# Moving the up phase's stores from SyncE's queue to the queues of GpSimd and ScalarE in a one-core decoder trunk

## The chip, the cores and the metric

The kernel runs on one core of a Trainium2 chip. A core has a matrix engine (TensorE, PE in the profile, with PEld for its weight loads), VectorE (DVE), ScalarE (ACT), GpSimd (POOL) and SyncE (SP), each working through its own list of instructions in order. Transfers between the chip's memory (HBM) and the on-chip buffer are DMAs. An engine issues one with an instruction in its own list, and the core's 16 DMA engines move the bytes. Engines wait for each other, and for DMAs, by semaphores: a waiting instruction holds all that stands behind it in its engine's list.

The metric is the device time of one execution in microseconds; smaller is better.

## The reference

One layer of a decoder trunk over 1024 positions of 1024 channels, in float32:

```python
h = layer_norm(x, ln_in_g, ln_in_b)
u = h @ w_in                       # conformer GLU | ssm z | ssm x,B,C | dt | gate_a | gate_b
y_a = conformer_branch(...)        # depthwise convolution of 31 taps
y_b = ssd_branch(...)              # Mamba-2, chunks of 128 positions
mix = (sigmoid(gate_a) * y_a + sigmoid(gate_b) * y_b) @ w_o
h = layer_norm(DN_ALPHA * h + mix, ln1_g, ln1_b)
# ConvFFN: the part that the change touches, and what follows it
u = causal_dwconv(h @ w_up, dw_w, dw_b)      # w_up (1024, 5632), 3 taps
gate, val = split(u, 2)
ffn = (silu(gate) * val) @ w_down            # w_down (2816, 1024)
h = layer_norm(DN_ALPHA * h + ffn, ln2_g, ln2_b)
```

## The kernel before

Each product runs as three float32r matmuls (`mm3`, lines 163 to 168), on a high part and a low part of each operand. So every weight tile that is loaded from HBM is first cast by ScalarE (the high part), then VectorE subtracts to give the low part, and only then can TensorE use it.

The kernel works in stages: the mixers and the combination for each half of the positions, the output projection, then the feed-forward network, in an up phase and a down phase.

*The up phase* (lines 1094 to 1107) makes 22 pairs of a gate and a value column block, numbered j. It saves multiplications: the positions and the channels are split in two, and each block product of 2 x 2 is made from seven smaller products. Two of the seven need only the first half of the positions and go ahead: `up_first(j)` (lines 806 to 814) multiplies with `b11` and then adds `b21` on top in the same accumulator. After each of the two, ScalarE copies the accumulator to a tile `first` (line 813; four such tiles) and line 814 stores it to HBM (`first_scr`). Eight such products run ahead (`LEAD`, line 1100); the other fourteen are strewn between the later ones. `up_rest(j)` (lines 839 to 907) makes the other five products:

- `up_weights` loads two raw weight tiles, `ra` and `rb` (lines 826 and 827), and VectorE makes sums of them.
- Lines 848 and 849 load the two stored products of `up_first(j)` again.
- ScalarE and VectorE bring together the partial results in `ug` and `uv` (lines 856 to 868), GpSimd clears their two leading columns (850 and 851), then the convolution of three taps and the gate follow in tiles of the tag `fo` (lines 870 to 896; three tiles).
- The result goes to HBM: for the lower eleven blocks the first half (line 899, 256 KB), for the upper eleven the whole tile (line 901, 512 KB) and two combinations of it with the lower block (lines 906 and 907, 512 and 256 KB).

*The down phase* (`down`, lines 909 to 1065) loads these tiles and the down weights again in steps (`load`): `dr` (lines 958 to 966) holds one step's operands, `c` (line 998) weights that are kept for later steps. The two rows of the last norm are loaded by line 203.

All DMAs, loads and stores alike, are issued by SyncE (`SY`).

*What sets the order.* The kernel is written in program order, but the list of each engine is laid out at build time by a planner (`schedule_with_timeline_sim`, line 1203). It goes forward in a modelled time with its own costs for every instruction, and gives an engine that is free the ready instruction of the highest priority. Priority is program order, with blocks moved ahead by `tc.high_priority(offset=...)`: weight loads and casts by 4000 or 2000 instructions (lines 150, 819, 955). Stores have no such offset. A tile's memory is given out again when its last reader is through, a store included. On the chip each list then runs in the planned order, whatever the real durations.

Of the kernel before, what the change touches and what calls it, by code (L numbers as in the profile page):

```python
# [55 lines left out]
def kernel(  # L56
# [15 lines left out]
    V, A, G, TE, SY = nc.vector, nc.scalar, nc.gpsimd, nc.tensor, nc.sync  # L72
# [14 lines left out]
    def bank(which):  # L87
        n_ps[0] += 1
        pl, tag = (pacc, "acc") if which else (psm, "sm")
        return pl.tile([P, 512], F32, tag=tag, name=f"{tag}{n_ps[0]}")  # L90
# [47 lines left out]
    first_scr = [dram.tile([2, P, HALF], F32, name=f"first_scr{j}") for j in range(NF)]  # L138
    NK = NF // 2
    b11_scr = [dram.tile([P, HALF], F32, name=f"b11_scr{k}") for k in range(NK)]  # L140
    t1_scr = [dram.tile([P, HALF], F32, name=f"t1_scr{k}") for k in range(NK)]
    b2_scr, t32_scr = (
        [dram.tile([P, T], F32, name=f"{n}_scr{k}") for k in range(NK)] for n in ("b2", "t32")
    )
# [4 lines left out]
    def weights(src, name, pl=None, eng=None, bufs=None):  # L149
        with tc.high_priority(offset=4000):  # L150
            st = wst.tile([P, D], F32, tag="st", name=f"st_{name}")
            SY.dma_start(st, src)
            w = (pl or wsp).tile([P, 2, D], F32R, tag="w", bufs=bufs, name=f"w_{name}")
            A.copy(w[:, 0, :], st)  # L154
            (eng or V).tensor_tensor(  # L155
                out=w[:, 1, :], in0=st, in1=w[:, 0, :].bitcast(F32), op=ALU.subtract
            )
        return w
# [557 lines left out]
    def product(ps, w, xs, first):  # L716

        for k in range(4):
            mm3(
                ps,  # L720
                lambda i: w(i)[:, k * P : (k + 1) * P],
                lambda i: xs(i)[:, k, :],
                first and k == 0,
                k == 3,
                not first,
            )
# [79 lines left out]
    def up_first(qp, bl, j):  # L806

        w = weights(wup[2 * j], f"ue{j}")
        ps = bank(1)
        for q, block in enumerate(("b11", "b21")):  # L810
            product(ps, lambda i: w[:, i, q * HALF : (q + 1) * HALF], bl[block], q == 0)
            f = qp.tile([P, HALF], F32, tag="first", bufs=4, name=f"first{q}_{j}")
            A.copy(f, ps)  # L813
            SY.dma_start(first_scr[j][q], f)

    def up_weights(upp, j):


        with tc.high_priority(offset=2000):
            r1, r2 = (  # L820
                wst.tile([P, D], F32, tag="st", name=f"r{n}{j}")
                if j % 2
                else upp.tile([P, D], F32, tag="raw", bufs=2, name=f"r{n}{j}")
                for n in "ab"
            )
            SY.dma_start(r1, wup[2 * j])
            SY.dma_start(r2, wup[2 * j + 1])
            a11, a12, a21, a22 = r1[:, :HALF], r1[:, HALF:], r2[:, :HALF], r2[:, HALF:]
            s3 = upp.tile([P, HALF], F32, tag="s3", name=f"s3_{j}")
            V.tensor_tensor(out=s3, in0=a11, in1=a21, op=ALU.add)  # L830
            V.tensor_tensor(out=a21, in0=a21, in1=a22, op=ALU.add)
            V.tensor_tensor(out=a11, in0=a21, in1=a11, op=ALU.add)
            V.tensor_tensor(out=a12, in0=a12, in1=a11, op=ALU.add)
            w24 = split_pair(wsp, r1, f"s24_{j}")
            w10 = split_pair(wsp, r2, f"s10_{j}")
            w3 = split_pair(upp, s3, f"s3_{j}", HALF, 2)
        return w24, w10, w3

    def up_rest(upp, bl, j, before):

        w24, w10, w3 = up_weights(upp, j)
        ug, uv = (
            upp.tile([P, T + 32], F32, tag="u", bufs=3, name=f"f{n}{j}") for n in ("ug", "uv")
        )
        s = upp.tile([P, HALF], F32, tag="s", bufs=2, name=f"s{j}")
        SY.dma_start(s, first_scr[j][0])
        SY.dma_start(ug[:, 2 : 2 + HALF], first_scr[j][1])
        G.memset(ug[:, :2], 0.0)  # L850
        G.memset(uv[:, :2], 0.0)
        ps, pz = bank(0), bank(0)
        early, late = slice(2, 2 + HALF), slice(2 + HALF, 2 + T)
        seeded = j > 1
        if seeded:
            A.copy(ps, s)
        product(ps, lambda i: w24[:, i, :HALF], bl["t2"], not seeded)
        if not seeded:
            V.tensor_tensor(out=ps, in0=s, in1=ps, op=ALU.add)
        A.copy(s, ps)  # L860
        product(pz, lambda i: w3[:, i], bl["t3"], True)
        product(ps, lambda i: w10[:, i, :HALF], bl["t1"], False)
        A.copy(uv[:, late], ps)  # L863
        V.tensor_tensor(out=uv[:, late], in0=pz, in1=uv[:, late], op=ALU.subtract)
        product(pz, lambda i: w10[:, i, HALF:], bl["t4"], False)
        V.tensor_tensor(out=uv[:, early], in0=pz, in1=s, op=ALU.subtract)
        product(ps, lambda i: w24[:, i, HALF:], bl["b22"], False)
        A.copy(ug[:, late], ps)
        os = []
        j = j // 2 + j % 2 * NK  # L870
        for jj, u in ((j, ug), (NF + j, uv)):
            o = upp.tile([P, T], F32, tag="o", bufs=3, name=f"fo{jj}")
            wc = PC_FW + 3 * jj
            A.activation(
                out=o, in_=u[:, 2 : 2 + T], func=AF.Identity, scale=pc[:, wc + 2 : wc + 3]
            )
            for k in range(2):
                V.scalar_tensor_tensor(
                    out=o,
                    in0=u[:, k : k + T],  # L880
                    scalar=pc[:, wc + k : wc + k + 1],
                    in1=o,
                    op0=ALU.mult,
                    op1=ALU.add,
                )
            os.append(o)
        og, ov = os
        A.activation(out=og, in_=og, func=AF.Silu, bias=pc[:, PC_FB + j : PC_FB + j + 1])
        V.scalar_tensor_tensor(
            out=ov,  # L890
            in0=ov,
            scalar=pc[:, PC_FB + NF + j : PC_FB + NF + j + 1],
            in1=og,
            op0=ALU.add,
            op1=ALU.mult,
        )
        early, late = slice(0, HALF), slice(HALF, T)
        if j < NK:
            SY.dma_start(b11_scr[j], ov[:, early])
            return ov  # L900
        SY.dma_start(b2_scr[j - NK], ov)
        a, b, t = before, ov, og
        V.tensor_tensor(out=t[:, early], in0=a[:, late], in1=b[:, late], op=ALU.subtract)
        V.tensor_tensor(out=a[:, late], in0=a[:, early], in1=a[:, late], op=ALU.subtract)
        V.tensor_tensor(out=t[:, late], in0=t[:, early], in1=a[:, early], op=ALU.subtract)
        SY.dma_start(t32_scr[j - NK], t)
        SY.dma_start(t1_scr[j - NK], a[:, late])

    def down(upp, dp, g, b):

# [183 lines left out]
    def firsts_to(n):  # L1094
        nonlocal n_first
        while n_first < min(n, NF):
            up_first(qp, bl, n_first)
            n_first += 1
# [5 lines left out]
    for j in range(NF):  # L1104
        firsts_to(LEAD + (j + 1) * (NF - LEAD) // (NF - 1))
        before = up_rest(upp, bl, j, before)
# [103 lines left out]
```

## Time and profile before

| | us |
|---|---|
| median of three runs (2031.75 to 2035.14) | 2033.81 |
| the profiled execution | 2034.61 |
| its span, first to last instruction | 2032.8 |
| TensorE busy | 1974.6 (97%) |
| VectorE busy | 1696.9 (83%) |
| ScalarE busy | 1031.2 (51%) |
| GpSimd busy | 147.3 (7%) |

The granted clock of TensorE is 0.991 of full speed on average. All DMAs together move 297.14 MB.

In the rows of the profile, `L814` is line 814 of the kernel; `SPq` is SyncE's queue, whose instructions issue DMAs and are not counted as busy. `first_scr<-first` names what is written and what is read. A row of a timeline gives the start (us from the span's start), the duration in us, the engine, the line, the operation, and how many were merged (x2); brackets hold the engine's idle time just before, and who ended it. A row of waits gives who waited for whom, the total in us, how many times, and the longest. The tiles `fo` are those of lines 872 to 896, `w_s` the cast weights of `up_weights`, `w_ue` those of `up_first`, `w_dn` those of the down phase. `b_scr` stands for `b11_scr` and `b2_scr`, `t_scr` for `t1_scr` and `t32_scr`.

### The profile page before, as it was taken

The numbers are of one execution on the slowest core, as the hardware profiler recorded it, in microseconds if no ns is written. First come the engines' busy times: TensorE is split into PE (matmuls) and PEld (weight loads), VectorE is DVE, ScalarE is ACT, GpSimd is POOL, SyncE is SP. The second block draws the span as 40 slices with busy tenths as digits, with TensorE's granted clock in tenths as the row PEclk, the third lists the DMA queues.
The fourth block names the chain that finished last, engine by engine and source line by source line (L and its number), as shares of the span: only waits on it lengthen the run. The fifth ranks groups of instructions, "written<-read, shape, count | busy, mean of one in ns | idle before, by whom it ended". The sixth has DMA issues, their size and how long they took to land.

```text
span 2032.8 us, 24888 instructions
## 1 busy us (share of the span) xinstructions
PE 1974.6 (97%) x9164; PEld 1624.8 (80%) x9164; DVE 1696.9 (83%) x2243; ACT 1031.2 (51%) x1489; POOL 147.3 (7%) x125
## 2 busy tenths in 40 slices
PE   6999999999999999999999999999999999979997
PEld 6888887888788888888888888887888888768865
DVE  7599999989766868999998976596788888879669
ACT  4465654556453265665454635264555555544323
POOL 2010101001400000100000131010000000000000
PEclk9999999999999999999999999999999999989999
DMA  6212233232545532222323253575455454775564
GB/s 219 93 63 94 78 102 106 99 104 100 165 129 197 203 106 75 88 84 84 122 86 114 98 170 126 182 247 208 158 169 191 163 190 166 277 289 184 161 210 147
DMA packets 110858, 297.14 MB, mean 146 GB/s; under 512 B 12560, under 2 KB 12560, under 8 KB 110736
## 3 DMA queue, kind: packets, MB, share of 16 engines
q1 hardware_dynamic: 110736, 295.55, 43.4%
q8 instruction: 72, 1.18, 0.3%
q14 instruction: 50, 0.41, 0.1%
HBM read 241.50 MB, written 54.00 MB: 145 GB/s over the span
## 4 chain that ended last, share of the span: by engine, by line
PE 72%; DVE 19%; DMA 5%; issue 3%; ACT 1%; SPq 0%; DVEq 0%; ACTq 0%
PE acc L166 16%; PE acc L168 16%; PE acc L167 16%; DVE c L420 6%; PE sm L166 5%; PE sm L168 5%; PE sm L167 5%; DMA dr<-wdown 2%; PE sm L534 2%; PE acc L357 1%; DVE xbc L375 1%; DVE w_dn L993 1%; PE sm L515 1%; DMA st_wo<-wo 1%; DMA dr<-b_scr 1%
## 5 line engine op out<-in xcount | busy, mean ns | idle before, releaser
L420 DVE SCALAR_TENSOR_TENSOR c<-v,pc,c 128x512 f32<-128x512 f32 x480 | 377.0, 810 | 6.8 <-ACT c L409 5.5
L478 POOL TENSOR_TENSOR au<-seg_mv,head_of 128x1024 fp32r<-128x1024 f32 x32 | 77.3, 2417 | 963.4 <-PE sm L487 728.4
L166 PE MATMUL acc<-hT,w_c 128*128 128x512 f32 x352 | 141.0, 401 | 0.0
L167 PE MATMUL acc<-hT,w_c 128*128 128x512 f32 x352 | 140.6, 399 | 0.0
L168 PE MATMUL acc<-hT,w_c 128*128 128x512 f32 x352 | 138.5, 393 | 0.0
L992 ACT CAST w_dn<-dr 128x1024 fp32r<-128x1024 f32 (+1 forms) x73 | 68.4, 945 | 112.0 <-DVE dr L930 58.2
L375 DVE SCALAR_TENSOR_TENSOR xbc<-u,pc,xbc 128x512 f32<-128x512 f32 x144 | 110.5, 780 | 0.7 <-ACT xbc L373 0.5
L166 PE MATMUL sm<-h1s,w_s 128*128 128x512 f32 x264 | 103.0, 390 | 1.4 <-ACT fuv L863 0.8
L167 PE MATMUL sm<-h1s,w_s 128*128 128x512 f32 x264 | 102.8, 389 | 0.0
L168 PE MATMUL sm<-h1s,w_s 128*128 128x512 f32 x264 | 102.8, 389 | 0.0
L167 PE MATMUL acc<-w_z,hT 128*128 128x512 f32 x256 | 100.9, 394 | 0.0
L166 PE MATMUL acc<-w_z,hT 128*128 128x512 f32 x256 | 100.8, 401 | 0.0
L168 PE MATMUL acc<-w_z,hT 128*128 128x512 f32 x256 | 100.7, 396 | 0.0
L154 ACT CAST w_c<-st_c 128x1024 fp32r<-128x1024 f32 x50 | 52.5, 1051 | 89.0 <-PE acc L168 68.3
L993 DVE TENSOR_TENSOR w_dn<-dr,w_dn 128x1024 fp32r<-128x1024 f32 (+1 forms) x73 | 78.6, 1091 | 13.3 <-ACT w_dn L992 12.7
L167 PEld LDWEIGHTS acc<-hT,w_c 128*128 128x128 f32 x352 | 66.1, 188 | 16.9 <-issue 3.8
L168 PEld LDWEIGHTS acc<-hT,w_c 128*128 128x128 f32 x352 | 66.1, 188 | 16.1 <-issue 2.6
L166 PEld LDWEIGHTS acc<-hT,w_c 128*128 128x128 f32 x352 | 66.1, 188 | 15.9 <-issue 2.6
L155 DVE TENSOR_TENSOR w_c<-st_c,w_c 128x1024 fp32r<-128x1024 f32 x47 | 60.7, 1291 | 20.3 <-ACT w_c L154 20.3
L166 PE MATMUL acc<-h1b,w_ue 128*128 128x512 f32 x176 | 69.8, 397 | 3.7 <-ACT first L813 3.7
L166 PE MATMUL acc<-w_dn 128*128 128x512 f32 x160 | 58.5, 397 | 12.1 <-ACT w_dn L992 12.1
L168 PE MATMUL acc<-h1b,w_ue 128*128 128x512 f32 x176 | 69.6, 399 | 0.0
(337 smaller groups left out, 5729.5 us busy)
## 6 DMA issues: line engine op xcount, KB each, us to landing
st_c<-wcol SPq DMA_DIRECT2D x50, 512.0 KB, 3.5
st_z<-wz SPq DMA_DIRECT2D x32, 512.0 KB, 3.4
dr<-wdown SPq DMA_DIRECT2D x55, 256.0 KB, 4.1
st_wo<-wo SPq DMA_DIRECT2D x24, 512.0 KB, 4.0
st_ue<-wup SPq DMA_DIRECT2D x22, 512.0 KB, 4.2
first_scr<-first SPq DMA_DIRECT2D x44, 256.0 KB, 2.3
ra<-wup SPq DMA_DIRECT2D x22, 512.0 KB, 3.6
rb<-wup SPq DMA_DIRECT2D x22, 512.0 KB, 3.7
```

The source lines that it names most:

```text
L154: A.copy(w[:, 0, :], st)
L155: (eng or V).tensor_tensor(out=w[:, 1, :], in0=st, in1=w[:, 0, :].bitcast(F32), op=ALU.subtract)
L166: TE.matmul(ps, wa(0), xa(0), start=start, stop=False, skip_group_check=more)
L167: TE.matmul(ps, wa(0), xa(1), start=False, stop=False, skip_group_check=more)
L168: TE.matmul(ps, wa(1), xa(0), start=False, stop=stop, skip_group_check=more)
L357: TE.matmul(ps[:, ts], w[:, i, k * P : (k + 1) * P], hT[:, j, k, ts], start=n == 0 and k == 0, stop=n == 2 and k == KD - 1,)
L375: V.scalar_tensor_tensor(out=o, in0=u[:, k : k + HALF], scalar=pc[:, wc + k : wc + k + 1], in1=o, op0=ALU.mult, op1=ALU.add,)
L420: V.scalar_tensor_tensor(out=accs[i], in0=v[:, k : k + HALF], scalar=pc[:, wc + k : wc + k + 1], in1=accs[i], op0=ALU.mult, op1=ALU.add,)
L478: G.tensor_tensor(out=au, in0=seg_mv[:, c, :].unsqueeze(1).to_broadcast([P, 8, P]), in1=head_of[:, g, :].unsqueeze(2).to_broadcast([P, 8, P]),
L534: TE.matmul(py[:, hs], m[:, h, :], xs[:, hs], start=True, stop=True)
L992: A.copy(w[:, 0, cs], src)
L993: V.tensor_tensor(out=w[:, 1, cs], in0=src, in1=w[:, 0, cs].bitcast(F32), op=ALU.subtract)
```

## The change

Five lines change the engine that issues a store, and nothing else in the text of the kernel. The store of a product that runs ahead is issued by ScalarE, which also makes the copy that it stores. The four stores of activations are issued by GpSimd. All loads stay on SyncE. Since the planner lays out all lists anew, the order of other instructions can change too.

```diff
@@ up_first @@
             A.copy(f, ps)
-            SY.dma_start(first_scr[j][q], f)
+            A.dma_start(first_scr[j][q], f)
@@ up_rest @@
         if j < NK:
-            SY.dma_start(b11_scr[j], ov[:, early])
+            G.dma_start(b11_scr[j], ov[:, early])
             return ov
-        SY.dma_start(b2_scr[j - NK], ov)
+        G.dma_start(b2_scr[j - NK], ov)
         a, b, t = before, ov, og
         V.tensor_tensor(out=t[:, early], in0=a[:, late], in1=b[:, late], op=ALU.subtract)
         V.tensor_tensor(out=a[:, late], in0=a[:, early], in1=a[:, late], op=ALU.subtract)
         V.tensor_tensor(out=t[:, late], in0=t[:, early], in1=a[:, early], op=ALU.subtract)
-        SY.dma_start(t32_scr[j - NK], t)
-        SY.dma_start(t1_scr[j - NK], a[:, late])
+        G.dma_start(t32_scr[j - NK], t)
+        G.dma_start(t1_scr[j - NK], a[:, late])
```

## The prediction

> **What bounds the kernel now.** I read the page first, then a table of windows over the phase that the change touches, then who TensorE waited for in it, then the timelines around each wait.
>
> ```profile
> span 2032.8 us, 24888 instructions
> PE 1974.6 (97%) x9164; PEld 1624.8 (80%) x9164; DVE 1696.9 (83%) x2243; ACT 1031.2 (51%) x1489; POOL 147.3 (7%) x125
> ...
> PE 72%; DVE 19%; DMA 5%; issue 3%; ACT 1%; SPq 0%; DVEq 0%; ACTq 0%
> ```
>
> TensorE is busy for 97% of the span, and the chain holds hardly any of SyncE's queue (SPq 0%). The up phase is the stretch from 1355 to 1800 us. Each window row gives its bounds and length, then the busy us (and instructions) of PE, PEld, DVE, ACT and POOL, the granted clock, the DMA share and GB/s.
>
> ```profile
> 1399.45:1403.20 3.75, 0.02 (x1) 0.00 (x0) 2.33 (x4) 1.59 (x3) 0.00 (x0) 0.78 0.89 344
> 1403.20:1408.60 5.40, 5.40 (x13) 4.32 (x14) 5.40 (x9) 2.60 (x3) 0.00 (x0) 0.52 0.28 104
> 1798.40:1809.75 11.35, 0.00 (x1) 0.00 (x1) 8.10 (x12) 1.04 (x1) 0.00 (x0) 0.61 1.05 390
> 1809.75:1814.80 5.05, 5.05 (x12) 4.00 (x13) 3.99 (x5) 1.99 (x2) 0.00 (x0) 0.52 1.04 398
> 1355.00:1800.00 445.00, 438.23 (x1921) 360.03 (x1919) 357.44 (x410) 239.97 (x312) 12.14 (x49) 0.99 0.55 188
> PE acc L166 <- ACT w_dn L992: 12.1, 2, 11.4
> PE acc L166 <- ACT first L813: 3.7, 1, 3.7
> PE sm L166 <- ACT fuv L863: 0.8, 1, 0.8
> PE sm L166 <- ACT s L860: 0.7, 1, 0.7
> ```
>
> (The last four are waits of TensorE: in all, times, longest.) TensorE loses time at two places only. Stall A, 1399.45 to 1403.20, costs 3.7 us, and the clock is then 0.52 for 5.40 us, another 5.40 x 0.48 = 2.6. Stall C, where the up phase meets the down phase, costs 11.4 us and 5.05 x 0.48 = 2.4. With the 1.5 us of the two small waits there is some 21.6 us, 1.1% of the span, that any change of this phase can win. Everything else is full: of the phase's 445.00 us TensorE lacks 6.8, and these are 3.7, 1.5 and the 1.6 of stall C that lie before 1800.
>
> **What the queue of SyncE holds back.** The stores sit in the loads' queue and wait there.
>
> ```profile
> SPq L814 <- ACT first L813: 88.6, 31, 7.3
> SPq L899 <- DVE fo L889: 30.0, 11, 11.2
> SPq L203 <- PE sm L168: 3.7, 1, 3.7
> SPq L827 <- DVE w_ue L155: 0.6, 1, 0.6
> ```
>
> (The last row is of 1385 to 1400 alone.) 88.6 + 30.0 = 118.6 us of waiting for stores look like a prize. But a wait in a queue costs only if the load behind it was ready. At stall A the order is this, in the timelines of SyncE, DVE, ACT and PE:
>
> ```profile
> 1390.64 0.81 SPq L814 DMA_DIRECT2D first_scr<-first  x2
> 1392.15 0.33 SPq L827 DMA_DIRECT2D rb<-wup  x1
> 1392.53 0.46 SPq L826 DMA_DIRECT2D ra<-wup  x1
> 1393.04 0.42 SPq L827 DMA_DIRECT2D rb<-wup  x1
> 1395.18 0.81 SPq L814 DMA_DIRECT2D first_scr<-first  x2
> 1390.91 1.22 DVE L155 TENSOR_TENSOR w_ue<-st_ue,w_ue 128x1024 fp32r<-128x1024 f32 x1
> 1400.83 0.69 DVE L830 TENSOR_TENSOR s<-ra,rb 128x512 f32<-128x512 f32 x1 [6.73 <-DMA rb<-wup]
> 1401.56 0.62 ACT L731 CAST w_s<-s 128x512 fp32r<-128x512 f32 x1 [5.92 <-DVE s L830]
> 1403.20 0.80 PE L166 MATMUL acc<-h1b,w_ue 128*128 128x512 f32 x1 [3.73 <-ACT first L813]
> ```
>
> The second rb comes late (1400.83). The DVE waits for it, ACT waits for the DVE with a cast that stands ahead of the `first` copy, and TensorE waits for that copy. The rb was issued behind another rb, which needed the DVE's L155: 1390.91 + 1.22 = 1392.13, and it left at 1392.15. The store at 1390.64 was through before that. So here the store held back nothing that I can show; the order of the loads did. Stall C, in the timeline of SyncE, with one row of the DVE:
>
> ```profile
> 1786.12 0.32 SPq L899 DMA_DIRECT2D b_scr<-fo  x1
> 1790.26 0.33 SPq L203 DMA_DIRECT2D ln_g<-prow  x1
> ...
> 1791.12 11.03 SPq L998 DMA_DIRECT2D c<-wdown  x16
> 1803.17 0.33 SPq L960 DMA_DIRECT2D dr<-wdown  x1
> ...
> 1807.97 0.33 SPq L901 DMA_DIRECT2D b_scr<-fo  x1
> 1802.80 1.28 DVE L889 SCALAR_TENSOR_TENSOR fo<-fo,pc,fo 128x1024 f32<-128x1024 f32 x1
> ```
>
> The store L899 blocks the queue for 11.2 us, but the next in line, L203, waits for TensorE until 1790.26 by itself. Then 16 loads of c stand ahead of the dr that TensorE needs, and they run at the DMA's rate (share 1.05, 390 GB/s). Taking L899 away frees an empty stretch.
>
> **The change, part by part.** The sum goes by the profiled run: 2034.61 us, its span of 2032.8 and 1.8 around it; the median of the three runs, 2033.81, lies 0.8 below.
>
> *SyncE loses 88 issues.* Forty-four of L814 and 11 each of L899, L901, L906 and L907, at the 0.32 us of the row at 1786.12: 28 us of issuing, and the waits above. By the two orders just shown I take a gain of 0. The bound is what the planner might do with the freed slots, 21.6 us; it is a rival below.
>
> *ACT gains 44 issues.* Nothing on ACT's queue issues a DMA today; the nearest row is SyncE's 0.32 us. 44 x 0.32 = 14.1 us, so ACT goes from 239.97 to some 254 of the 445 us. Behind a `first` copy ACT mostly waits for TensorE:
>
> ```profile
> 1490.52 0.59 ACT L813 COPY first<-acc 128x512 f32<-128x512 f32 x1 [0.76 <-PE acc L168]
> 1493.31 0.59 ACT L863 COPY fuv<-sm 128x512 f32<-128x512 f32 x1 [2.21 <-PE sm L168]
> 1531.33 1.16 ACT L874 ACTIVATE fo<-fug,pc 128x1024 f32<-128x1024 f32 x1 [0.93 <-DMA b_scr<-fo]
> 1532.95 1.06 ACT L731 CAST w_s<-rb 128x1024 fp32r<-128x1024 f32 x1 [0.46 <-PE sm L168]
> 1534.31 1.06 ACT L154 CAST w_ue<-st_ue 128x1024 fp32r<-128x1024 f32 x1 [0.30 <-PE acc L168]
> ACT fo L874 <- DMA b_scr<-fo: 4.4, 4, 1.9
> L478 POOL TENSOR_TENSOR au<-seg_mv,head_of 128x1024 fp32r<-128x1024 f32 x32 | 77.3, 2417 | 963.4 <-PE sm L487 728.4
> 1385.36 2.01 DVE L155 TENSOR_TENSOR w_ue<-st_ue,w_ue 128x1024 fp32r<-128x1024 f32 x1
> 1385.00 1.30 POOL L785 TENSOR_TENSOR ts<-h1raw,ts 128x512 f32<-128x512 f32 x1 [4.66 <-DVE h1s L755]
> ```
>
> The first two rows show it: 2.21 us of waiting stand behind that copy, more than an issue. I take 0. If that cover is gone, the 16 stores of the eight products that run ahead (lines 1100 and 1101) pay 16 x 0.32 = 5.1, the upper bound; below 0 it can't go, since ACT only gets work. Queued behind each store are ACT's next copies and casts, and TensorE behind them.
>
> *GpSimd gains 44 issues.* It is busy 12.14 of 445 us, so the place is free; its memsets of L850 and L851 now stand behind stores that wait for the DVE, as they wait for the DVE already. No row shows a DMA issued by GpSimd. Bounds: SyncE's 0.32, and the dearest GpSimd instruction here, L478 at 2.42. Who waits for such a store is ACT's L874, whose slot of `fo` the store frees: 4.4 us in four waits. After the one that ended at 1531.33 ACT waits again 0.46 + 0.30 = 0.76 us, so a store later by x costs about x - 0.76 at each of the four. At 2.42 this is 4 x (2.10 - 0.76) = 5.4; at 0.32, nothing. A gain is excluded: the stores wait for the DVE (rows L899 above), and GpSimd can't run ahead of that. I take a price of 1.3, nearer to the smaller row since an issue moves no tile: 4 x (0.98 - 0.76) = 0.9.
>
> The Trainium skill (DMA: Bandwidth & Descriptors, Specifications) gives a first-byte latency of about 1 us on the GpSimd path and 0.6 on the others; by that the store is 0.4 later and the term would be 0.
>
> *The stores get queues of their own beside the loads.* Today the pair at 1395.18 stands behind the late rb. From another queue it may share with it. A 256 KB store takes 0.262 MB / 390 GB/s = 0.67 us, so rb comes up to 1.34 us later, and stall A grows as much; if the queue keeps the order, 0. I take 1.3, since all engines are near full there (share 0.89). In C the last 512 KB store (1.34 us) can leave when L889 is through, 1802.80 + 1.28 = 1804.08 instead of 1807.97, and can push the awaited dr, issued at 1803.17; bounds 0 and, with its fellows of 256 and 512 KB, 3.4. I take 1.0, as part of the dr is through by then.
>
> The Trainium skill speaks of this (DMA: Bandwidth & Descriptors, Queues, rings and completion order): each DMA engine goes round between the queues it has work for, packet by packet. By it the 1.3 and the 1.0 are real, without it they would be 0 and the sum 2.3 lower; no run here has shown a second queue.
>
> **Sum:** 2034.6 + 0 + 0 + 0.9 + 1.3 + 1.0 = 2037.8; less the 0.8 to the median, 2037.0 us. That is +0.16%; a measurement of this kernel can tell about 0.2%, 4 us, from no change.
>
> **The rivals.**
> *Faster: the planner uses the freed queue.* The order on each engine is planned at build time, and 88 entries less on SyncE can bring rb or the dr ahead of what delays them. For it speaks that 16 loads of c stand ahead of one dr that TensorE waits for; against it that loads already have priority over stores. If A goes: 2033.8 - 6.3 = 2027.5. If C goes too, 2033.8 - 6.3 - 13.8 = 2013.7. It decides from 4 us won, two thirds of A.
> *Slower: GpSimd's stores land late.* L874 stands on ACT ahead of the casts that feed TensorE. The DVE works 357.44 of 445 us, and its L155 took 2.01 instead of 1.22 beside the GpSimd operation of 1385.00, so the two do get in each other's way. A store that waits out two operations like L889 is later by x = 0.98 + 2 x 1.28 = 3.5, and the four places cost 4 x 2.74 = 11.0 instead of 0.9: 2047. It decides from x = 1.2 (4 x 0.46 = 1.8, 0.9 more than the forecast has). Against it: no row shows it for a DMA, which reads no tile on GpSimd. The Trainium skill (SBUF — State Buffer, SBUF: two separate sides) has the rule that would do this: while the DVE runs an operation in a 2-port mode, GpSimd can't write a DMA's descriptors.
> *Slower: the new plan is worse.* ACT in order with 44 more entries, and waits in front of them, puts casts later; one more stall like A, with its slow clock, costs 6.3: 2037.0 + 6.3 = 2043. Against it: ACT has 205 us free in the phase.
>
> **How the numbers follow.** Forecast and its neighbourhood 2031 to 2041: 0.46. Faster plan: 0.22. Late GpSimd stores: 0.14. Worse plan: 0.18. Faster by over 0.2% (below 2029.7) is the first rival and a little of the forecast, 0.23; within, most of the forecast, 0.35; slower (above 2037.9) the two slow rivals and a quarter of the forecast's chance, 0.42. The range runs from 2018, part of C won, to 2050, two stalls like A added; the forecast's own is 2031 to 2041.
>
> **What would show it.** SyncE's waits for L813 and L889 gone; ACT's busy time for L813 as before, with 0.3 to 0.5 us behind each; the wait of L874 for `b_scr` above 4.4 us; stall A still there with rb as its cause, and 16 loads of c still ahead of the dr. Wrong it would be if stall A or C is gone, or if TensorE has a wait of over 2 us between 1410 and 1760.

## The result, and the profile after

The changed kernel takes 2036.35 us (median of 20 runs), the kernel before, run in turn with it, 2032.49 (20 runs). The ratio is 1.0019 with a 95% interval of 1.0010 to 1.0027: some 3.9 us slower (2.0 to 5.5). The kernel before was run anew beside each group of experiments, and its median differs between the groups by up to 1.7 us. So each comparison below is a ratio to the runs of its own group, turned into us with 2034.

From the page of the changed kernel (its profiled execution took 2038.49 us): the span, the busy times, and the DMA queues with their packets, MB and share.

```profile
span 2036.8 us, 24876 instructions
PE 1976.3 (97%) x9164; PEld 1624.5 (80%) x9164; DVE 1694.6 (83%) x2243; ACT 1030.8 (51%) x1489; POOL 170.5 (8%) x169
q1 hardware_dynamic: 98064, 266.71, 38.1%
q0 software_dynamic: 4928, 17.30, 2.2%
q10 hardware_dynamic: 6336, 11.54, 1.5%
```

The change did what it says: 17.30 MB now leave by GpSimd's queue and 11.54 MB by ScalarE's, and GpSimd has 44 instructions more (169 for 125). TensorE is busy 1976.3 us, 1.7 more than before, with the same 9164 matmuls: of the 3.9 us of span 1.7 are slower matmuls and 2.2 new waits. Who TensorE waited for, in the changed kernel from 1340 us to the end of the span:

```profile
PE acc L166 <- ACT w_dn L992: 12.8, 3, 11.2
PE sm L167 <- DVE w_dn L993: 4.4, 3, 2.3
PE acc L166 <- ACT first L813: 3.1, 1, 3.1
PE acc L167 <- DVE w_dn L993: 2.1, 2, 1.3
```

Stall C (L992, 11.2) and stall A (L813, 3.1) stand as before. The two small waits for L860 and L863 are gone. What has grown are the waits for L993, VectorE's subtraction in the down phase. The same two rows of the kernel before, from 1812 us on:

```profile
PE sm L167 <- DVE w_dn L993: 2.4, 2, 1.3
PE acc L167 <- DVE w_dn L993: 0.8, 1, 0.8
```

To see where the 4 us arise I cut each trace at the same matmuls. Both kernels run 9164 of them, so the start of the 6600th marks nearly the same point of the work in each. The table gives the us between such starts; it is worked out from the traces, and the names of the columns say what lies there.

```
                6300-6600  6600-8100  8100-8200  8200-8340  8340-8460  8460-8880  8880-9100
                 stall A    up phase   its end    stall C    order      down       down
before             70.75      341.48     24.69      45.65      27.21      95.31      58.81
after              69.93      341.53     22.67      47.03      31.44      96.83      58.04
x1_first           67.46      341.58     24.71      45.22      27.65      96.97      58.75
x2_act             70.37      343.20     22.67      46.94      31.47      99.22      58.30
x3_after_k1        71.38      341.52     22.67      47.41      28.17      97.16      58.85
x4_before_k6       69.83      341.52     24.71      45.68      31.46      96.89      58.88
x5_k1_last         69.87      341.53     22.67      47.01      28.18      96.31      59.63
x6_before_c        71.01      341.45     24.71      38.96      35.00      95.20      58.65
x7_after_c         70.74      341.56     22.67      40.37      32.65      95.26      59.17
x8_after_c_par     65.83      341.45     24.69      39.25      35.35      95.43      60.22
x9_before_par      64.83      341.49     24.69      45.04      28.18      96.63      58.47
x10_first_par      64.74      341.45     24.69      45.27      28.19      97.13      58.20
x11_after_par      64.70      341.54     24.71      46.09      28.18      95.61      57.92
```

After against before: stall A -0.8, the end of the up phase -2.0, stall C +1.4, then +4.2 in one stretch of 120 matmuls, +1.5, -0.8. With +0.3 from the work ahead of the first column, which the change does not touch, and less than 0.1 in all elsewhere, that is the 3.9 us by which the spans differ. Each row is one execution. Two columns vary by themselves: the first between 67.5 and 71.4 in kernels that all have stall A (its wait took 2.7 to 4.4 us), the sixth between 95.2 and 97.2 in most (x1_first has 1.7 more than before there, with the same lists on TensorE and VectorE). What the first shows below 4 us, and the sixth below 2, is not put down to a cause. The work ahead of the first column varies as well: it ends between 1338.7 and 1343.1 us.

The stretch with +4.2, in the timelines of VectorE and TensorE of the changed kernel:

```profile
1831.40 1.23 DVE L993 TENSOR_TENSOR w_dn<-dr,w_dn 128x1024 fp32r<-128x1024 f32 x1
1832.55 1.28 DVE L1014 SCALAR_TENSOR_TENSOR rows<-rows,acc 128x512 f32<-128x512 f32 x2
1833.74 0.68 DVE L930 TENSOR_TENSOR c<-c,dr 128x512 f32<-128x512 f32 x1
1834.35 0.68 DVE L930 TENSOR_TENSOR c<-c,c 128x512 f32<-128x512 f32 x1
1834.95 1.22 DVE L993 TENSOR_TENSOR w_dn<-dr,w_dn 128x1024 fp32r<-128x1024 f32 x1
1836.22 0.50 PE L167 MATMUL sm<-w_dn 128*128 128x512 f32 x1 [2.31 <-DVE w_dn L993]
```

And two windows of the changed kernel from there (columns as in the prediction's windows):

```profile
1835.00:1840.00 5.00, 3.78 (x11) 2.98 (x12) 5.00 (x8) 0.42 (x1) 0.00 (x0) 0.72 0.43 150
1840.00:1845.00 5.00, 5.00 (x22) 4.10 (x21) 5.00 (x9) 2.64 (x3) 0.00 (x0) 0.94 0.30 96
```

The subtraction that TensorE waits for runs from 1834.95 to 1836.17, and 0.05 us later the matmul starts. The wait is 2.31 us; the clock behind it is 0.72 and 0.94, which by an estimate from these two windows costs another 5 x 0.28 + 5 x 0.06 = 1.7. Together that is 4.0 of the 4.2. In the kernel before, VectorE's timeline shows its subtractions at almost the same times:

```profile
1831.70 1.23 DVE L993 TENSOR_TENSOR w_dn<-dr,w_dn 128x1024 fp32r<-128x1024 f32 x1
1835.24 1.23 DVE L993 TENSOR_TENSOR w_dn<-dr,w_dn 128x1024 fp32r<-128x1024 f32 x1
```

The rows look alike, 1831.40 and 1834.95 against 1831.70 and 1835.24. The names in full, in the planned lists, tell them apart (`w_dn1_6` is block 6 of the second of the seven products):

```
VectorE, L993, before:  w_dn1_2  w_dn1_4  w_dn1_1  w_dn1_6  w_dn1_3
VectorE, L993, after:   w_dn1_2  w_dn1_4  w_dn1_6  w_dn1_1  w_dn1_3
TensorE, both:          w_dn1_0  w_dn1_1  w_dn1_2  w_dn1_3  ...
```

The planner put the cast and the subtraction of `w_dn1_6` ahead of those of `w_dn1_1`, which TensorE needs five blocks earlier. What in its modelled time turned them is not known. Further on other pairs are turned too (`w_dn1_7` and `w_dn1_8`, `w_dn1_9` and `w_dn1_10`, and those of the next product); the pair shown is the first. Had `w_dn1_1` had the first place, it would have been there at 1832.63, before TensorE came for it at 1836.22 - 2.31 = 1833.91.

### The profile page after: what moved, and what is told of

It is laid out like the page before. It is cut to its first block, busy times and chain, and to the rows that moved or that the text cites. A ratio compares the mean times of both kernels' runs of the same rounds, so it can differ in the third digit from the quotient of the medians.

```text
span 2036.8 us, 24876 instructions
## 1 busy us (share of the span) xinstructions
PE 1976.3 (97%) x9164; PEld 1624.5 (80%) x9164; DVE 1694.6 (83%) x2243; ACT 1030.8 (51%) x1489; POOL 170.5 (8%) x169
## 3 DMA queue, kind: packets, MB, share of 16 engines
q0 software_dynamic: 4928, 17.30, 2.2%
q10 hardware_dynamic: 6336, 11.54, 1.5%
## 4 chain that ended last, share of the span: by engine, by line
PE 65%; DVE 23%; DMA 6%; issue 4%; ACT 1%; SPq 0%; DVEq 0%; ACTq 0%
PE acc L168 14%; PE acc L166 14%; PE acc L167 14%; DVE c L420 8%; PE sm L167 5%; PE sm L168 5%; PE sm L166 5%; DMA dr<-wdown 2%; DVE xbc L375 2%; PE acc L357 1%; PE sm L534 1%; DVE w_dn L993 1%; DMA r<-h_scr 1%; PE sm L515 1%; DVE w_so L155 1%
## 5 line engine op out<-in xcount | busy, mean ns | idle before, releaser
L992 ACT CAST w_dn<-dr 128x1024 fp32r<-128x1024 f32 (+1 forms) x73 | 68.0, 945 | 115.6 <-DVE dr L930 46.0
L993 DVE TENSOR_TENSOR w_dn<-dr,w_dn 128x1024 fp32r<-128x1024 f32 (+1 forms) x73 | 78.5, 1088 | 9.9 <-ACT w_dn L992 9.1
L155 DVE TENSOR_TENSOR w_c<-st_c,w_c 128x1024 fp32r<-128x1024 f32 x47 | 60.6, 1289 | 20.2 <-ACT w_c L154 20.2
```

The costliest lines, as they stand in the source:

```text
L155: (eng or V).tensor_tensor(out=w[:, 1, :], in0=st, in1=w[:, 0, :].bitcast(F32), op=ALU.subtract)
L992: A.copy(w[:, 0, cs], src)
L993: V.tensor_tensor(out=w[:, 1, cs], in0=src, in1=w[:, 0, cs].bitcast(F32), op=ALU.subtract)
```

## The experiments

Theory P (plan): the loss is this order, which came about because the planner laid out all lists anew. Theory S (stores): the stores' own queues take DMA time from loads that are waited for, and VectorE falls behind. Theory I: issuing costs ScalarE time. In kernels with lines added above them, the cast and the subtraction of the down phase are L997 and L998 instead of L992 and L993. The ranges in us that were expected of the first four kernels were reckoned from a before of some 2032.5; beside these four it took 2034.18, so some 1.7 us have to be added to each range.

### Each half of the change alone: x1_first and x2_act

```diff
 x1_first, from the kernel before:
-            SY.dma_start(first_scr[j][q], f)
+            A.dma_start(first_scr[j][q], f)
 x2_act, from the kernel before:
-            SY.dma_start(b11_scr[j], ov[:, early])
+            G.dma_start(b11_scr[j], ov[:, early])
 ... (and the stores to b2_scr, t32_scr and t1_scr)
```

> Only the 44 stores of first products leave SyncE (for ScalarE); the activation stores stay. The lists of TensorE and VectorE are those of before, and the down phase's casts stand in before's order. Theory P (the loss is the new plan of the down phase, the cast of w_dn1_6 put ahead of that of w_dn1_1): no such order here, so no wait of TensorE for L993 at 1833; time at or a little below before, 2029 to 2033 us, since of the up phase only the small gains seen in the changed kernel are left. Theory S (stores beside loads are what costs): the stores of L814 share the DMA with loads, 2033 to 2036, stall A at least as long as before (3.7 us). Theory I (issuing costs ScalarE): up to 5 us above before.

> Only the 44 activation stores leave SyncE (for GpSimd). The casts of the down phase stand in the changed kernel's order (w_dn1_6 ahead of w_dn1_1). Theory P: the whole loss is here, 2035.5 to 2038, with a wait of TensorE for L993 of some 2.3 us near 1833 and a lowered clock behind it. Theory S: about half of the loss, 2033 to 2036. Theory I: as before, 2031 to 2034.

Measured: x1_first 0.9997 (0.9988 to 1.0006), so -0.6 us (-2.4 to +1.2); x2_act 1.0015 (1.0007 to 1.0024), +3.1 us (1.4 to 4.9). Theory I falls: 44 issues on ScalarE cost nothing that can be seen. P had x1_first at or a little below before; its median of 2034.16 lies in P's range so moved, and not in S's. The time of x2_act alone, 2037.17, doesn't tell the whole loss from half of it. The loss comes with the activation stores on GpSimd. TensorE's longest wait of x2_act in that stretch, in its timeline:

```profile
1835.98 0.50 PE L167 MATMUL sm<-w_dn 128*128 128x512 f32 x1 [2.31 <-DVE w_dn L993]
```

And ScalarE's DMA issues in x1_first, in the view of line 814 (count; least, median and most in ns; first and last start):

```profile
L814 ACTq DMA_DIRECT2D first_scr<-first x44: 326/326/932, 1361.4 to 1754.3; - x44
```

x2_act has the changed kernel's order and its wait of 2.31 us to the hundredth; its column "order" reads 31.47, x1_first's 27.65. In the planned lists the order also turns when only the stores of the upper eleven blocks move, and not when only those of the lower eleven do. But P and S both allow that these stores cost. The next two separate them.

### The order alone: x3_after_k1 and x4_before_k6

An edge between two instructions of one engine fixes their order in its list; no wait and no work is added. But the planner lays out anew what stands behind the pair: in x4_before_k6 the later pairs turn as in the changed kernel, in x3_after_k1 they turn back, and some loads behind them change places. So what these two change is the order of this part of the lists, from the pair on.

```diff
 x3_after_k1, from the changed kernel, in load():
                 for cs, src in cuts:
+                    behind = made.get((1, 1) if (p, k) == (1, 6) else None, ())
+                    (each ins of behind:) es.enter_context(tc.issue_after(ins.ins))
-                    A.copy(w[:, 0, cs], src)
-                    V.tensor_tensor(...)
+                    hi = A.copy(w[:, 0, cs], src)
+                    lo = V.tensor_tensor(...)
+                    made[p, k] = (hi, lo)
 x4_before_k6, from the kernel before: the same edge turned round,
 cast and subtraction of w_dn1_1 behind those of w_dn1_6
```

> The changed kernel with one edge of order more on ScalarE and on VectorE: the cast and the subtraction of w_dn1_6 stand behind those of w_dn1_1; all stores as in the changed kernel. Theory P: the wait of 2.3 us at 1833 and the 1.8 us of slow clock behind it go, 2031 to 2032.5 us, not above before. Theory S: the dr still land late behind GpSimd's stores (8.4 us from issue instead of 5.3), VectorE still idles 4.1 us at 1810 to 1814, and the time stays at 2035 to 2037.

> The kernel before, all stores on SyncE, with the opposite edge: the cast and the subtraction of w_dn1_1 stand behind those of w_dn1_6. Theory P: the order alone costs, 2034.5 to 2037 us, with a wait of TensorE for the subtraction of w_dn1_1 of 1.4 us or more near 1835. Theory S: VectorE has no arrears here, 2032 to 2033.

Measured: x4_before_k6 1.0021 (1.0012 to 1.0030), +4.3 us (2.4 to 6.1). x3_after_k1 1.0009 (1.0000 to 1.0018), +1.8 us (0 to 3.7). TensorE's wait at the first matmul that needs the low part of `w_dn1_1`, in the timeline of x4_before_k6:

```profile
1835.15 0.50 PE L167 MATMUL sm<-w_dn 128*128 128x512 f32 x1 [2.31 <-DVE w_dn L998]
```

And of x3_after_k1 the same matmul, then the next one that waits, 24 matmuls later:

```profile
1832.56 0.40 PE L167 MATMUL sm<-w_dn 128*128 128x512 f32 x1
1838.84 0.50 PE L167 MATMUL sm<-w_dn 128*128 128x512 f32 x1 [0.66 <-DVE w_dn L998]
```

x4_before_k6 settles that the order is enough: no store has moved, and it has the wait of 2.31 us, a column "order" of 31.46 and all of the loss. That is what P had foreseen (its median of 2038.97 is 0.3 above P's range so moved); S had foreseen no change. In x3_after_k1 the wait is gone and the column falls from 31.44 to 28.17, so the order is what costs in the changed kernel too. But its median of 2036.28 did not come to the level of before as P had it. It lies between the two theories, though its interval begins at level, and S's mechanism is there in the trace:

```
us from issue to landing of the dr that stand next in SyncE's list
after        issued 1804.43 to 1806.40 (four):  6.7  8.0  8.4  8.4   GpSimd's stores issued 1803.53, 1806.07, 1806.90
before       issued 1805.28 to 1807.24 (four):  5.3  5.0  5.3  5.3   SyncE's store L901 issued 1807.97, behind them
x3_after_k1  issued 1802.99 to 1804.96 (four):  7.3  8.5  8.4  8.4
```

### The last block's stores back on SyncE: x5_k1_last

```diff
 from x3_after_k1, and the same for t32_scr and t1_scr:
-        G.dma_start(b2_scr[j - NK], ov)
+        (G if j < NF - 1 else SY).dma_start(b2_scr[j - NK], ov)
```

> The changed kernel with the edge of x3_after_k1, and the three stores of the last column block (b2, t32, t1; 1.25 MB) issued by SyncE again, so that they stand behind loads in one queue. Theory P+S (the order costs 4.2 us; what x3 still had above before, 1.8 us, is VectorE falling behind because these three stores push the awaited dr): the dr issued at about 1805 land after 5.3 instead of 8.4 us, VectorE idles 1 us instead of 4 at 1810 to 1814, and the time comes to 2031 to 2034, level with before or 1 us below. Rival U (the rest sits in the up phase or is the run's own variation): the dr land sooner, but the time stays 1.5 to 2.5 us above before.

Measured: 0.9998 (0.9987 to 1.0009), -0.4 us (-2.6 to +1.8). VectorE's timeline at the place in question, in the changed kernel:

```profile
1814.21 1.35 DVE L930 TENSOR_TENSOR c<-c,dr 128x512 f32<-128x512 f32 x2 [4.09 <-DMA dr<-wdown]
```

And in x5_k1_last:

```profile
1811.79 1.34 DVE L930 TENSOR_TENSOR c<-c,dr 128x512 f32<-128x512 f32 x2 [1.09 <-DMA dr<-wdown]
```

The four dr now land after 5.3 to 5.4 us, and VectorE waits 1.09 instead of 4.09. So the stores in a queue of their own do push the loads by 3 us, as S says. That this reaches the time is not shown: the columns "stall C" and "order" of x5_k1_last (47.01, 28.18) are those of x3_after_k1 (47.41, 28.17), and the other differences between these two lie in the two columns that vary by themselves. The intervals of the two kernels overlap; a cost of the late dr of some 2 us (1.8 against -0.4) stays open. What is settled is that the changed kernel with its order mended and these three stores put back is level with the kernel before within that interval.

### Stall C: x6_before_c and x7_after_c

The prediction counted stall C as 13.8 us to be won, because 16 loads of c stand ahead of one dr. These two put each load of c behind the dr of its own step.

```diff
 x6_before_c from the kernel before, x7_after_c from the changed one:
+                    weight = SY.dma_start(w_st, ...)      (the dr of this step)
-                SY.dma_start(c, (a21, a22)[p])
+                    es.enter_context(tc.issue_after(weight.ins))
+                    SY.dma_start(c, (a21, a22)[p])
 ... (the two rows of the last norm are loaded behind the dr of step 12)
```

> The kernel before (all stores on SyncE), but each load of c is issued behind the loads of dr of its own step, and the two rows of the last norm behind the dr of step 12. Stall C is then short: after the first loads of c and one addition the awaited dr is issued near 1797 instead of 1802.5. If 16 loads of c ahead of one dr make stall C, TensorE waits 2 to 6 us there instead of 11.4, and the time is 2022 to 2028. If the store L899, which holds SyncE until TensorE is through, makes it, stall C stays at 11 us and the time at 2032 to 2035. In this plan the cast of w_dn1_6 stands ahead of that of w_dn1_1 again, which by x4_before_k6 can take 4 of it back.

> The same edit of the c loads in the changed kernel. Stall C 2 to 6 us; the cast of w_dn1_1 stands ahead of w_dn1_6 in this plan. 2021 to 2028 us: if the stores' own queues help once the loads are in the right order, 1 to 4 us below x6_before_c; if the last stores push the dr, above it.

Measured: x6_before_c 0.9997 (0.9986 to 1.0008), x7_after_c 0.9995 (0.9984 to 1.0005). Nothing won, where 2022 to 2028 and 2021 to 2028 us were expected: the shorter stall came as expected, the time did not. TensorE's waits from 1795 to 1850 us in x6_before_c:

```profile
PE acc L166 <- ACT w_dn L992: 4.7, 1, 4.7
PE sm L166 <- ACT w_dn L992: 2.6, 1, 2.6
PE sm L167 <- DVE w_dn L993: 2.1, 1, 2.1
```

And three windows of x6_before_c:

```profile
1810.00:1820.00 10.00, 10.00 (x45) 8.26 (x44) 9.42 (x13) 3.17 (x3) 0.00 (x0) 1.00 1.04 398
1820.00:1830.00 10.00, 7.87 (x35) 6.19 (x33) 7.98 (x12) 3.73 (x4) 0.00 (x0) 1.00 1.04 394
1830.00:1840.00 10.00, 7.42 (x20) 5.61 (x21) 10.00 (x15) 2.56 (x3) 0.00 (x0) 0.66 0.95 334
```

Stall C does fall from 11.4 to 4.7 us, so the order of the loads made it where it stood, and the store L899 did not (it is still on SyncE here). But 4.7 us of new waits come 25 us later. "Stall C" wins 6.7 and "order" loses 7.8. Part of the 7.8 is the turned order of `w_dn1_6`, which this plan has too; x7_after_c has the right order, wins 6.7 against the changed kernel's stall C and still reads 32.65 in the next column. The DMA share is 1.04 up to 1830, and 1.02 to 1.05 from 1800 to 1830 in the kernel before: the loads of c are due in this stretch either way, and at this rate they only change places. That the rate of the DMA bounds the stretch is how I read these rows; no run took bytes away.

### Stall A: x8_after_c_par to x11_after_par

The prediction put stall A down to an rb issued behind another rb. The tiles of block 0 come from a pool that is free only once the stage before is through, those of block 1 from the pool that L155 frees, and block 1's loads stand first. The edit exchanges the pools.

```diff
 in up_weights():
-                if j % 2
+                if j % 2 == 0
 x8_after_c_par:  x7_after_c with it
 x9_before_par:   the kernel before with it and with the edge of x3_after_k1
 x10_first_par:   x1_first with both
 x11_after_par:   x5_k1_last with it
```

> x7_after_c, and in addition the raw weight tiles of the even column blocks come from the pool that the odd ones used, and the other way round, so that the tiles of block 0 wait for VectorE's L155 and not for the last use of the stage before. If stall A is made by the place of these loads in the queue, it goes (3 to 6 us with the slow clock behind it), 2016 to 2024 us; if the loads only change places, the time is that of x7_after_c, within 2 us.

> All stores on SyncE as in the kernel before; the pools of the raw weight tiles are exchanged between even and odd column blocks, and the edge that keeps the cast of w_dn1_1 ahead of w_dn1_6 is set. If stall A is a matter of which pool the tiles of block 0 come from, as x8 says, and the stores' queue has no part in it, it goes here too (3.7 us and 1 to 2 us of slow clock): 2028 to 2030 when before is at 2034. If the change is needed for it, stall A stays and the time is 2032 to 2035.

> As x9_before_par, with the stores of the first products issued by ScalarE. By x1_first (no difference) level with x9_before_par, within 1.5 us. If the stores in SyncE's queue hold loads back once stall A is gone, 2 us or more below it.

> The changed kernel with the edge, with the last block's three stores on SyncE, and with the exchanged pools: 2028 to 2030, level with x9_before_par within 1.5 us, since without the new order of the down phase the moved stores were worth nothing (x5_k1_last). If they are worth something once stall A is gone, 2 us or more below x9_before_par.

Measured: x8_after_c_par 0.9970 (0.9959 to 0.9981), -6.1 us. x9_before_par 0.9975 (0.9965 to 0.9985), x10_first_par 0.9977 (0.9969 to 0.9986), x11_after_par 0.9975 (0.9966 to 0.9985): -5.1, -4.7 and -5.1 us. All four are faster than the kernel before. The 2016 to 2024 us expected of x8_after_c_par were reckoned from a gain of x7_after_c that did not come. The medians of x10_first_par and x11_after_par lie 1.8 and 1.2 us above that of x9_before_par, their ratios 0.4 and 0; the first is just outside the 1.5 us expected, but the intervals overlap for the most part. From the timelines of x9_before_par, SyncE's issue of block 0's rb and VectorE's first addition of `up_weights`:

```profile
1386.54 0.33 SPq L827 DMA_DIRECT2D rb<-wup  x1
1393.15 0.68 DVE L830 TENSOR_TENSOR s<-ra,rb 128x512 f32<-128x512 f32 x1
```

And all of TensorE's waits in x9_before_par from 1340 us on for something other than `w_dn`:

```profile
PE sm L166 <- ACT fuv L863: 0.8, 1, 0.8
PE sm L166 <- ACT s L860: 0.7, 1, 0.7
PE acc L168 <- DVE w_ue L155: 0.2, 1, 0.2
```

The rb leaves at 1386.54 instead of 1393.04, the addition has no wait in its brackets, and the wait for L813 is gone. The first column falls to 64.83, 5.9 below before and 2.6 below the lowest of the kernels with the stall; the prediction had priced stall A at 6.3. In x9_before_par every store is on SyncE. So the stall came from the place of these loads and not from the stores in their queue. And with the stall gone, one half of the moved stores (x10) or nearly all of them (x11) are worth as much as none.

## Why the prediction came out as it did

The time was forecast at 2037.0 and came at 2036.35, inside the forecast's own range and, at +0.19%, just within the bound of 0.2%, where the prediction saw a chance of 0.35 (0.42 for slower than that). The sum has the right size for a wrong reason: three terms of contention that add to 3.2 us stand where one misplaced pair of instructions costs 4.2. That the two are nearly the same is luck.

- *SyncE's 88 issues gain 0.* Right. x1_first takes 44 of them away and wins nothing, x9_before_par keeps all of them and wins 5.1. The waits of SyncE for L813 and L889 are gone from the changed kernel, stalls A and C are not. SyncE now waits in other places instead (12.2 us at L203).
- *ACT's 44 issues cost 0.* Right; one takes 0.33 us, as estimated from SyncE's 0.32.
- *GpSimd's price, +0.9.* Mis-sized. It was taken as 1.3 us; a GpSimd issue is busy for 0.54 us, and the 256 KB store lands 0.3 us later than from SyncE, as the row of DMA issues of the kernel before shows (KB each, median us to landing):

```profile
b_scr<-fo SPq DMA_DIRECT2D x11, 256.0 KB, 2.0
```

  and that of the changed kernel:

```profile
b_scr<-fo POOLq DMA_DIRECT2D x11, 256.0 KB, 2.3
```

  Who waits for such a store is ACT's L874. Its waits in the changed kernel, from 1340 to 1800 us:

```profile
ACT fo L874 <- DMA b_scr<-fo: 3.3, 3, 1.2
```

  This was to rise above 4.4 and fell to 3.3, so the term is 0. The lower price was the one that went with the Trainium skill (DMA: Bandwidth & Descriptors, Specifications), whose 0.4 us between the two paths is near the 0.3 measured. The rival of late GpSimd stores falls with it: of the 11 issues of L899 none took more than 0.71 us, and none of these stores landed later than 3.2 us (3.1 before), so none waited out an operation like L889 (1.28). (The rival's 4 x 0.46 at x = 1.2 should read 4 x 0.44; its 1.8 stands.)
- *Stall A, +1.3.* Not seen: 3.1 us with ScalarE's queue, 3.7 without, within a spread of 2.7 to 4.4. The awaited rb took 7.1 us from issue to landing (6.8 in x1_first), against 7.8 before, so the stores beside it did not lengthen it.
- *Stall C, +1.0.* The mechanism was there, the place of its cost wrong. The last stores do push dr, by 3 us, which agrees with the round robin that the Trainium skill states (DMA: Bandwidth & Descriptors, Queues, rings and completion order). But the first dr, which ends stall C, is not among them (5.4 us from issue to landing in both kernels), and the stall stays at 11.2 us, so the term is 0 there. VectorE idles 3 us more behind it, and no cost of that is shown. The column's +1.4 is a wait of 1.1 us at 1783 that the new plan has in place of the two small waits of 1763 to 1768.
- *The step that failed is the new plan at nothing in the sum.* The prediction had it only as the third rival, "the new plan is worse", with a chance of 0.18, and looked for it on ACT in the up phase, as a consequence of 44 more entries there. It came in the down phase, 27 us after the last moved store (1806.90 to 1833.91), in casts and subtractions that the change does not name, and was set off by the stores on GpSimd. Its price, a stall and its slow clock, was of the right kind: 4.2 against 6.3. The profile of the kernel before could not exclude it.
- *"21.6 us that any change of this phase can win".* Right for stall A (6.3 priced, 5.9 in the column and 5.1 in the time of x9_before_par), wrong for stall C: 6.7 us of it can be moved and none was won (x6, x7).

## What to carry to other kernels

Where a planner lays out the lists, an edit of one queue can move instructions far from it: compare the planned order of every engine, in the order in which the bound engine consumes the tiles, before looking for contention. A queue that waits a lot is no prize; ask whether the load behind the wait was ready. Before counting a stall that ends with a late load as a gain, look whether the DMA has room in the stretch behind it. Here the stall with a share of 1.04 on both sides only moved (stall C), and the one with 0.28 behind it was won (stall A); that the share is the reason is argued, not shown.

## What the runs showed of the hardware

Three stores, 1.25 MB in all, in a second queue lengthened loads of 256 KB in the first from 5.3 to 8.4 us, though some of these loads were issued ahead of two of the stores. With the same stores behind the loads in one queue (x5_k1_last) the loads took 5.3 to 5.4. GpSimd's issue takes 0.54 us of its own time for 256 and 512 KB alike, with VectorE busy for 80% of the phase; SyncE's and ScalarE's take 0.32 to 0.33. A wait of TensorE of 2.31 us was followed by a granted clock of 0.72 over 5 us (changed kernel); behind one of 0.66 us it stayed at 1.00 (x3_after_k1, 1836 to 1846).
